# FFN stages that end on VectorE alone, and new engine costs in the planner that orders a Trainium2 kernel

## The chip, the cores and the metric

The kernel runs on one core of a Trainium2 chip. A core has five engines, each with an instruction queue of its own that it works off in order: TensorE (PE in the profile), VectorE (DVE), ScalarE (ACT), GpSimd (POOL) and SyncE (SP, which issues the transfers). The metric is the device time of one execution in microseconds, the median of several runs.

## The reference, cut to what matters

Four residual stages over a sequence of 1024 positions with 1024 features, all in float32: an FFN, a token mixer (two kinds of causal softmax attention), a second FFN, and then two layers on the sequence with 16 positions put ahead of it, an "even" layer (RG-LRU and SSD) and an "odd" one (stick-breaking attention).

```python
def swiglu(x, w_gate, w_up, w_down):
    return (jax.nn.silu(x @ w_gate) * (x @ w_up)) @ w_down      # 1024 -> 2816 -> 1024
...
f1 = swiglu(rms_norm(x, ffn1_pre_g[l]), ffn1_w_gate[l], ffn1_w_up[l], ffn1_w_down[l])
x = x + FFN_RESIDUAL_WEIGHT * rms_norm(f1, ffn1_post_g[l])
m = token_mixer(rms_norm(x, mix_pre_g[l]), w_in[l], ...)
x = x + rms_norm(m, mix_post_g[l])
f2 = swiglu(rms_norm(x, ffn2_pre_g[l]), ffn2_w_gate[l], ffn2_w_up[l], ffn2_w_down[l])
x = x + FFN_RESIDUAL_WEIGHT * rms_norm(f2, ffn2_post_g[l])
...
log_keep = jnp.where(before, jax.nn.log_sigmoid(-z), 0.0)       # odd layer, a block of 128 queries
csum = jnp.cumsum(log_keep, axis=-1)
weights = jnp.where(before, jnp.exp(jax.nn.log_sigmoid(z) + csum[..., -1:] - csum), 0.0)
```

## The kernel before, in words

Each float32 operand of a large product is split into a high and a low part (`wh` and `wl`, `Ah` and `Al`, `dh` and `dl`): ScalarE copies the high part, and another engine subtracts it for the low part. Three matmuls, lines 336 to 338 in `mm3`, then make one product.

The order of the instructions in every queue is decided while the program is built. Pieces of work are Python generators, called threads, which ask for an engine ("P", "A", "V", "G" for GpSimd, "D" for transfers) and give a cost in microseconds. `Sched.run` takes, again and again, the request with the smallest start time, then the smallest priority. The costs come from the functions `pe`, `act`, `dve` and `pool_tt`, and `HOP`, 0.45, is what it adds when work passes from one engine to another. So these numbers are no instructions; they decide which row stands ahead of which on each engine.

- **FFN stage** (`ffn_stage`, called twice). The products go by a seven-product scheme: `down` runs the products p of each chunk ci (0 to 2), with the result in `pdn` in PSUM. `evac_d` adds it into eight accumulators `acc` of 128x1024 (line 1104), some of the adds on GpSimd. `split_d` (line 1049) makes `dl`, the low parts of down's left operands. When an accumulator is complete, `post` takes its squares on ScalarE, gets `rs_y`, the inverse root, by small operations of 128x2 on VectorE (lines 306 to 310), multiplies by the gain `gp` (line 1220 in `scale`, on GpSimd for six of the eight, or line 1212) and adds the residual rows `xs` (line 1209, or 1215). `rows.put` stores the tile. The tiles are then normalized (line 603), transposed (`ptf`) and split into the next stage's `Ah` and `Al` (line 542).
- **`ahead`** is the stream that splits the next stage's first weights during an FFN's end; its subtraction (line 473 in `Stream.split`) is on GpSimd.
- **Mixer, even and odd stage.** Projections (`pe`, `pq`, `pk`, `pv`, `pg`) and attention or SSD chunks are emitted as threads beside each other, so that matmuls of the former stand between the waits of the latter. In the odd stage a block goes from scores `psc` (line 1500) over a scan of `kt` (line 2219), a product (line 2223), transposes `ptr` (line 1560) and their split `th`, `tl` (line 1511) to `po` (line 1543). In the even stage a chunk of the SSD goes from transposes `psx` to `xd` and `ab` on VectorE (lines 2703 and 2725), then to `psy`, `pso` and `pst` on TensorE; `sz` is a gate made from the projection `pe`. Outputs are projected by `pwo`.

Of the kernel before, what the change touches and what calls it, by code (L numbers as in the profile page):

```python
# [13 lines left out]
ALU = mybir.AluOpType  # L14
# [8 lines left out]
L = M + S  # L23
# [73 lines left out]
def act(n):  # L97
    return 0.07 + 0.92e-3 * n


def dve(n, speed=1):
    return 0.08 + 1.045e-3 * n / speed


def pool_tt(n):
    return 0.2 + 2.1e-3 * n

# [549 lines left out]
def ffn_stage(c, A, first, rows0, wg, wu, wd, gpost, res, rows, nxt, meta=None, cols=None):  # L657
# [6 lines left out]
    nc, tc, sch = c.nc, c.tc, c.sch  # L664
# [5 lines left out]
    with ExitStack() as ctx:  # L670
# [418 lines left out]
        def evac_d(ci, p, t, ps):  # L1089
# [22 lines left out]
            if p == 1:  # L1112
                if ci == 0:
                    yield from copy(c00, ps)
                    v = c01
                else:
                    yield from add(c00, c00)
                    v = yield from new_sg()
                vs[t] = v
                tt = yield from copy(v, ps)  # L1120
            elif p == 2:
                tt = yield from add(c00, c00)
            elif p == 6:
                v = vs[t]
                tt = yield from add(v, v)
            elif p == 7:
                v = vs[t]
                if ci == 0:
                    tt = yield from add(c10, v)
                else:  # L1130
                    yield from add(c01, c01, "G", v)
                    tt = yield from add(v, v)
            elif p == 4:
                tt = yield from add(c10, c10)
            elif p == 5:
                yield from add(c11, c11)
                tt = yield from add(c01, c01)
            else:
                tt = yield from add(c01, c01)
            r_mm.release(tt)  # L1140
            if p == 7:
                if ci == 0:
                    tt = yield from copy(c11, c10)
                else:
                    eng = "V" if ci == 2 else "G"
                    yield from add(c10, c10, eng, v)
                    tt = yield from add(c11, c11, "G", v)
                    r_sg.release(tt)
# [36 lines left out]
        def post(t, done):  # L1185
# [3 lines left out]
            nc.scalar.activation(junk(), acc[t], AF.Square, accum_out=ss[g][:, t - g:t - g + 1])  # L1189
            scaled = Ev()  # L1190
            on_pool = t not in (5, 7)
            if on_pool:
                sch.spawn(scale(t, scaled), 1, tt)
            left[g] = left.get(g, len(rows.members(t))) - 1
# [9 lines left out]
            r = rs[g][:, t - g:t - g + 1]  # L1204
            if on_pool:
                yield scaled
                yield ev_x[t]
                yield ("V", dve(1024))
                nc.vector.scalar_tensor_tensor(acc[t], acc[t], r, xs[t], op0=ALU.mult, op1=ALU.add)
            else:  # L1210
                yield ("V", dve(1024))
                nc.vector.scalar_tensor_tensor(acc[t], acc[t], r, gp[0], op0=ALU.mult, op1=ALU.mult)
                yield ev_x[t]
                yield ("V", dve(1024))
                nc.vector.tensor_add(acc[t], acc[t], xs[t])
            yield from rows.put(t, acc[t], junk)

        def scale(t, ev):
            t_ = yield ("G", pool_tt(1024))
            nc.gpsimd.tensor_mul(acc[t], acc[t], gp[0])  # L1220
            ev.set(t_)

# [74 lines left out]

        ahead = Stream(c, "G", shared=True)
        ahead.r_hl.free.clear()
# [417 lines left out]
def mixer_stage(c, A, rows0, prm, w_in, forget_b, lams, subln, rope, w_out, gpost, res, rows):  # L1717
# [3 lines left out]
    with ExitStack() as ctx:  # L1721
# [18 lines left out]
        def gate_evac(lf, tok, ps):  # L1740
# [17 lines left out]
            if tok is HALVES[1]:  # L1758
                cum = pm.tile([8, S], F32, tag="bc", name="cum", bufs=2)
                yield ("V", dve(1024))  # L1760
                nc.vector.tensor_tensor_scan(cum, c.one[:8].to_broadcast([8, S]), lf, 0.0, op0=ALU.mult, op1=ALU.add)
                t = yield ("D", 0.3)
                nc.sync.dma_start(cD, cum)
                r_bc.release(t + 1.0)
                r_bc.release(t + 1.0)
                T.event("cum").set(t + 2.0)
# [132 lines left out]
        def softmax(segs, m, pt, cb, ev, r):  # L1899
# [3 lines left out]
            for s, ps in enumerate(segs):  # L1903
                yield ("V", dve(m))
                if cb is not None:
# [7 lines left out]
            for s, ps in enumerate(segs):  # L1913
                t = yield ("A", act(m))
                nc.scalar.activation(pt[:, s * m:s * m + m], ps[:, :m], AF.Exp, bias=mx[:, 0:1], scale=-1.0,
                                     accum_out=sm[:, s:s + 1])
                T.r_ps["sc"].release(t)
            yield ("V", 0.2 * ns)
            if ns == 2:
# [214 lines left out]
def odd_stage(c, A, rows0, prm, w_in, w_out, res, final, out):  # L2134
# [3 lines left out]
    with ExitStack() as ctx:  # L2138
# [68 lines left out]
        def weights(ps, w, kt, k0, m, before, scanned, done):  # L2207
# [8 lines left out]

            t = yield ("V", dve(m))
            rev = kt[:, k0:k0 + m][:, ::-1]
# [224 lines left out]
def even_stage(c, A, rows0, prm, w_in, lru_wa, lru_wx, dt_bias, a_log, ssd_d, w_out, meta, res, rows):  # L2443
# [168 lines left out]
    def dt_rest():  # L2612
# [21 lines left out]
        nc.vector.tensor_scalar(l, dt, na, None, op0=ALU.mult)  # L2634
        yield ("V", dve(L))
        nc.vector.tensor_tensor_scan(ac, cut, l, 0.0, op0=ALU.mult, op1=ALU.add)
# [287 lines left out]
    def lru_rest(b, h, r, ig, t_, v):  # L2924
# [31 lines left out]
        for j in range(2):  # L2956
            u = 2 * b + j
            t = yield ("V", dve(LH, 0.5))
            nc.vector.tensor_tensor_scan(t_[:, j], r[:, j], v[:, j], 0.0 if h == 0 else carry[:, u:u + 1], op0=ALU.mult,
# [286 lines left out]
```

## Time and profile before

| | |
|---|---|
| median of 3 runs | 3675.97 us (3673.99 to 3686.52) |
| the profiled execution | 3678.58 us, span of its trace 3676.9 us |
| mean granted clock of TensorE | 0.978 of full speed |
| first FFN | 0 to about 705 us |
| mixer | to about 1350 us |
| second FFN | to about 2049 us |
| even stage | to about 2850 us |
| odd stage | to the end |

The span is the time from the first instruction to the last; 1.7 us of the run's time lie outside it. The stages follow one another, with the end of one over the start of the next. Since TensorE has most of the work, what matters of another engine is where TensorE stands still for it.

### The profile page before, as it was taken

The page shows a single profiled execution, that of the slowest core. Times are in us where ns is not written, and L with a number is a line of the kernel's source. Part 1 is how long each engine was busy: PE and PEld are TensorE (multiplying, and loading weights), DVE is VectorE, ACT ScalarE, POOL GpSimd, SP SyncE. Part 2 cuts the span into 40 slices and gives each one's busy share as a digit, 9 for nine tenths or more (in the row PEclk, how much of TensorE's full clock was granted, in tenths as well). Part 3 has the DMA queues.
Part 4 walks back from the last instruction along what each step waited for, and adds up shares of the span by engine and source line. Part 5 has one row for each costly group of instructions (what it writes and reads, how often), then busy time and mean ns, then how long its engine had stood idle before and what let it go on. Part 6 is the DMA issues. An engine that isn't in the chain of part 4 may idle for free. (4 is left out here: it accounts for less than half of the span.)

```text
span 3676.9 us, 51971 instructions
## 1 busy us (share of the span) xinstructions
PE 3469.4 (94%) x19675; PEld 2950.4 (80%) x19675; DVE 2756.6 (75%) x4900; ACT 1694.3 (46%) x3449; POOL 641.5 (17%) x577
## 2 busy tenths in 40 slices
PE   8899999799999899999999899998999999999989
PEld 7688888578878777888887899988878888888867
DVE  7876699977888769766799768568623788878784
ACT  4333244455656643333344437446412565656561
POOL 3211145411110114211354112113100000000000
PEclk9999999899999999999999999999999999999999
DMA  4232372311210342332561334234332111110123
GB/s 147 87 108 100 120 264 69 128 53 43 68 51 28 104 154 82 106 109 89 183 215 52 111 70 79 68 84 87 119 116 92 55 35 30 30 35 26 35 82 104
DMA packets 296627, 332.52 MB, mean 90 GB/s; under 512 B 17620, under 2 KB 220544, under 8 KB 296376
## 3 DMA queue, kind: packets, MB, share of 16 engines
q1 hardware_dynamic: 290584, 308.15, 27.6%
q10 hardware_dynamic: 5792, 21.04, 1.5%
q8 instruction: 155, 2.54, 0.3%
q14 instruction: 96, 0.79, 0.1%
HBM read 250.80 MB, written 78.35 MB: 90 GB/s over the span
## 5 line engine op out<-in xcount | busy, mean ns | idle before, releaser
L336 PE MATMUL pe<-Ah,wh 128*128 128x260 f32 (+1 forms) x1184 | 344.1, 291 | 21.6 <-ACT sz L224 7.5
L338 PE MATMUL pe<-Ah,wl 128*128 128x260 f32 (+1 forms) x1184 | 339.3, 287 | 0.0
L337 PE MATMUL pe<-Al,wh 128*128 128x260 f32 (+1 forms) x1184 | 339.0, 287 | 0.0
L224 ACT CAST wh<-w 128x512 fp32r<-128x512 f32 x280 | 162.5, 619 | 271.1 <-PE pst L337 193.0
L892 DVE TENSOR_TENSOR sg<-sg,pst 128x512 f32<-128x512 f32 x280 | 186.5, 682 | 114.6 <-PE pst L338 114.3
L337 PE MATMUL pst<-Al,wh 128*128 128x512 f32 x640 | 253.4, 396 | 2.2 <-DVE Al L815 2.2
L473 DVE TENSOR_TENSOR wl<-w,wh 128x512 fp32r<-128x512 f32 x280 | 209.9, 772 | 58.9 <-ACT wh L224 57.5
L336 PE MATMUL pst<-Ah,wh 128*128 128x512 f32 x640 | 251.8, 393 | 0.0
L338 PE MATMUL pst<-Ah,wl 128*128 128x512 f32 x640 | 251.6, 393 | 0.0
L337 PE MATMUL pdn<-dl,dh 128*128 128x512 f32 x592 | 233.4, 394 | 16.3 <-DVE dl L1049 16.3
L336 PEld LDWEIGHTS pe<-Ah,wh 128*128 128x128 f32 (+1 forms) x1184 | 225.8, 191 | 26.0 <-ACT sz L224 8.0
L1511 DVE TENSOR_TENSOR tl<-ptr,th 128x512 fp32r<-128x512 f32 (+2 forms) x344 | 198.0, 592 | 63.6 <-ACT th L224 61.2
L224 ACT CAST th<-ptr 128x512 fp32r<-128x512 f32 (+2 forms) x344 | 170.7, 515 | 133.4 <-PE ptr L1560 128.2
L338 PE MATMUL pdn<-dh,dl 128*128 128x512 f32 x592 | 231.7, 391 | 0.0
L336 PE MATMUL pdn<-dh 128*128 128x512 f32 x592 | 231.6, 391 | 0.0
L956 POOL TENSOR_TENSOR h<-h 128x512 f32<-128x512 f32 x88 | 134.5, 1529 | 535.6 <-DVE h L938 530.5
L337 PEld LDWEIGHTS pe<-Al,wh 128*128 128x128 f32 (+1 forms) x1184 | 225.7, 191 | 1.5 <-issue 0.5
L338 PEld LDWEIGHTS pe<-Ah,wl 128*128 128x128 f32 (+1 forms) x1184 | 225.5, 191 | 0.8
L2219 DVE TENSOR_TENSOR_SCAN kt<-kt,onec 128x392 f32<-128x392 f32 (+6 forms) x224 | 202.5, 914 | 26.1 <-ACT kt L224 25.0
L224 ACT CAST wh<-wr 128x1024 fp32r<-128x1024 f32 (+2 forms) x116 | 119.0, 1026 | 212.0 <-PE pwo L3045 121.7
L473 DVE TENSOR_TENSOR wl<-wr,wh 128x1024 fp32r<-128x1024 f32 (+1 forms) x110 | 138.8, 1263 | 86.0 <-ACT wh L224 85.7
L336 PE MATMUL pst<-T,wh 128*128 128x512 f32 x480 | 188.4, 395 | 10.9 <-ACT T L224 10.8
(555 smaller groups left out, 10496.0 us busy)
## 6 DMA issues: line engine op xcount, KB each, us to landing
hD<-h SPq DMA_DIRECT2D x22, 1792.0 KB
w<-in_ffn_w_gate_dram SPq DMA_DIRECT2D x20, 1024.0 KB
w<-in_ffn_w_up_dram SPq DMA_DIRECT2D x20, 1024.0 KB
d<-hD SPq DMA_DIRECT2D x18, 1024.0 KB
wr<-in_even_w_in_dram SPq DMA_DIRECT2D x36, 512.0 KB
wr<-in_odd_w_in_dram SPq DMA_DIRECT2D x32, 512.0 KB
wr<-in_w_in_dram SPq DMA_DIRECT2D x24, 512.0 KB
d<-in_ffn_w_down_dram SPq DMA_DIRECT2D x8, 1024.0 KB
```

What stands on the lines that cost most here:

```text
L224: self.last = _o(*a, **k)
L336: nc.tensor.matmul(ps, wh, xh, start=start, stop=False)
L337: nc.tensor.matmul(ps, wh, xl, start=False, stop=False)
L338: nc.tensor.matmul(ps, wl, xh, start=False, stop=stop)
L473: (nc.gpsimd if eng == "G" else nc.vector).tensor_sub(lo, raw, hi.bitcast(F32))
L892: nc.vector.tensor_add(dst, src, ps)
L956: nc.gpsimd.tensor_sub(q[:, o], q[:, a], q[:, b_])
L1511: nc.vector.tensor_sub(tl[:rows, :n], ptr[:rows, :n], th[:rows, :n].bitcast(F32))
L2219: nc.vector.tensor_tensor_scan(rev, rev, c.one.to_broadcast([P, m]), kt[:, k0 + m:k0 + m + 1], op0=ALU.mult, op1=ALU.mult)
```

## The change

The functions that give costs have new numbers, and the scans get a function of their own. At the end of both FFN stages no work is given to GpSimd: all eight tiles of `post` go the way that two went before, the adds of chunk 2 at p=7 go to VectorE, and so does the subtraction of `ahead`. The planner then runs with the new costs, so that the order of nearly all stages is another.

```diff
 def act(n):
-    return 0.07 + 0.92e-3 * n
+    return 0.16 + 0.87e-3 * n


 def dve(n, speed=1):
-    return 0.08 + 1.045e-3 * n / speed
+
+    return (0.15 if speed == 1 else 0.21) + 1.05e-3 * n / speed
+
+
+def scan(n):
+    return 0.22 + 2.08e-3 * n
+
+
+ACCUM = 0.19


 def pool_tt(n):
-    return 0.2 + 2.1e-3 * n
+    return 0.2 + 2.6e-3 * n
...
             elif p == 7:
                 v = vs[t]
+                eng = "V" if ci == 2 else "G"
                 if ci == 0:
                     tt = yield from add(c10, v)
                 else:
-                    yield from add(c01, c01, "G", v)
+                    yield from add(c01, c01, eng, v)
                     tt = yield from add(v, v)
...
                 else:
-                    eng = "V" if ci == 2 else "G"
                     yield from add(c10, c10, eng, v)
-                    tt = yield from add(c11, c11, "G", v)
+                    tt = yield from add(c11, c11, eng, v)
...
-            scaled = Ev()
-            on_pool = t not in (5, 7)
-            if on_pool:
-                sch.spawn(scale(t, scaled), 1, tt)
...
-            if on_pool:
-                yield scaled
-                yield ev_x[t]
-                yield ("V", dve(1024))
-                nc.vector.scalar_tensor_tensor(acc[t], acc[t], r, xs[t], op0=ALU.mult, op1=ALU.add)
-            else:
-                yield ("V", dve(1024))
-                nc.vector.scalar_tensor_tensor(acc[t], acc[t], r, gp[0], op0=ALU.mult, op1=ALU.mult)
-                yield ev_x[t]
-                yield ("V", dve(1024))
-                nc.vector.tensor_add(acc[t], acc[t], xs[t])
+            yield ("V", dve(1024))
+            nc.vector.scalar_tensor_tensor(acc[t], acc[t], r, gp[0], op0=ALU.mult, op1=ALU.mult)
+            yield ev_x[t]
+            yield ("V", dve(1024))
+            nc.vector.tensor_add(acc[t], acc[t], xs[t])
             yield from rows.put(t, acc[t], junk)
-
-        def scale(t, ev):
-            t_ = yield ("G", pool_tt(1024))
-            nc.gpsimd.tensor_mul(acc[t], acc[t], gp[0])
-            ev.set(t_)
...
-        ahead = Stream(c, "G", shared=True)
+        ahead = Stream(c, "V", shared=True)
...
-            t = yield ("V", dve(m))
+            t = yield ("V", scan(m))
             rev = kt[:, k0:k0 + m][:, ::-1]
             nc.vector.tensor_tensor_scan(rev, rev, c.one.to_broadcast([P, m]), kt[:, k0 + m:k0 + m + 1],
                                          op0=ALU.mult, op1=ALU.mult)
```

The other scans (`cum` of the mixer, `ac` and the LRU's `t_` of the even stage) get `scan` in the same way, and the softmax of the mixer has 0.14, `ACCUM` and 0.16 in its costs. By the order, GpSimd has 548 instructions instead of 582, VectorE 4920 instead of 4886, ScalarE three ACT table loads more (58), all in the even stage, and TensorE 19667 as before.

The first place is VectorE at the first FFN's end, where the last `dl` and the first tiles' `post` stand. Before:

```order
L308 SCALAR_TENSOR_TENSOR rs_a<-rs_y 128x2
L309 TENSOR_TENSOR rs_a<-rs_a,rs_v 128x2
L310 SCALAR_TENSOR_TENSOR rs_y<-rs_a,rs_y 128x2
L1209 SCALAR_TENSOR_TENSOR acc<-acc,rs_y,gp 128x1024
L1049 TENSOR_TENSOR dl<-d,dh 128x512
L308 SCALAR_TENSOR_TENSOR rs_a<-rs_y 128x2
L1209 SCALAR_TENSOR_TENSOR acc<-acc,rs_y,gp 128x1024
L1104 TENSOR_TENSOR acc<-acc,pdn 128x512
L309 TENSOR_TENSOR rs_a<-rs_a,rs_v 128x2
L1049 TENSOR_TENSOR dl<-d,dh 128x512
L310 SCALAR_TENSOR_TENSOR rs_y<-rs_a,rs_y 128x2
L1104 TENSOR_TENSOR acc<-acc,pdn 128x512
```

And of the change:

```order
L318 SCALAR_TENSOR_TENSOR rs_y<-rs_a,rs_y 128x2
L316 SCALAR_TENSOR_TENSOR rs_a<-rs_y 128x2
L1112 TENSOR_TENSOR acc<-acc,pdn 128x512
L317 TENSOR_TENSOR rs_a<-rs_a,rs_v 128x2
L1210 SCALAR_TENSOR_TENSOR acc<-acc,rs_y,gp 128x1024
L318 SCALAR_TENSOR_TENSOR rs_y<-rs_a,rs_y 128x2
L1210 SCALAR_TENSOR_TENSOR acc<-acc,rs_y,gp 128x1024
L1213 TENSOR_TENSOR acc<-acc,gp 128x1024 x2
L1210 SCALAR_TENSOR_TENSOR acc<-acc,rs_y,gp 128x1024 x2
L1213 TENSOR_TENSOR acc<-acc,d 128x1024 x2
L314 TENSOR_SCALAR rs_v<-ss 128x2
L1112 TENSOR_TENSOR acc<-acc,pdn 128x512 x4
```

The multiply by `gp` and the add of the residual are now two rows each on VectorE (L1210 and L1213) where GpSimd's product was ahead of one; the last `dl` (L1057) stands ahead of all of `post`. Behind these rows, up to the first `Al`, the order has two `wl` splits of 128x1024 and one of 128x64 that were GpSimd's, and one L1210 of a fifth tile.

The second place is TensorE in the even stage, at late chunks of the SSD (`psy`, `pso`, `pst` of one chunk, `psb` and `psx` of the next). Before:

```order
L2750 MATMUL psy<-ab,xd 64x128 x8
L2758 MATMUL pso<-xc_20290,S_21873 128x128 x4
L2763 MATMUL pst<-xe,bt 128x512
L2685 MATMUL psb<-xc_20290,xc_20113 128x128
L2686 MATMUL psb<-ident,xc_20113 128x128
L2691 MATMUL psx<-ident,xc_20748 128x128
L2691 MATMUL psx<-ident,xc_20749 128x128
L2691 MATMUL psx<-ident,xc_21656 128x128
L2691 MATMUL psx<-ident,xc_21657 128x128
L336 MATMUL pe<-Ah,wh 128x260
L337 MATMUL pe<-Al,wh 128x260
L338 MATMUL pe<-Ah,wl 128x260
```

And of the change:

```order
L2743 MATMUL psy<-ab,xd 64x128 x5
L2751 MATMUL pso<-xc_20276,S_21900 128x128 x4
L2756 MATMUL pst<-xe,bt 128x512
L2678 MATMUL psb<-xc_20276,xc_19962 128x128
L2679 MATMUL psb<-ident,xc_19962 128x128
L2684 MATMUL psx<-ident,xc_20824 128x128
L2684 MATMUL psx<-ident,xc_20825 128x128
L2684 MATMUL psx<-ident,xc_21652 128x128
L2684 MATMUL psx<-ident,xc_21653 128x128
L2743 MATMUL psy<-ab,xd 64x128 x8
L2751 MATMUL pso<-xc_20276,S_21900 128x128 x4
L2756 MATMUL pst<-xe,bt 128x512
```

Before, a chunk is followed by 48 rows of projections `pe` until the next `psy`; now the next chunk's `psy` stands right behind its `psx`, and so does the one after it.

The third place is TensorE in the odd stage, at the last projection `pg` of the kernel. Before:

```order
L338 MATMUL pg<-Ah,wl 128x512
L336 MATMUL pg<-Ah,wh 128x512
L337 MATMUL pg<-Al,wh 128x512
L338 MATMUL pg<-Ah,wl 128x512
L1543 MATMUL po<-th,v_31824 128x256
L1543 MATMUL po<-tl,v_31824 128x256
L1560 MATMUL ptr<-ident,pt 128x128 x3
L1543 MATMUL po<-th,v_31824 128x256
L1543 MATMUL po<-tl,v_31824 128x256
L1543 MATMUL po<-th,v_31824 128x256
L1543 MATMUL po<-tl,v_31824 128x256
L1500 MATMUL psc<-ks_32630,qs_25472 128x328
```

And of the change:

```order
L344 MATMUL pg<-Ah,wh 128x512
L345 MATMUL pg<-Al,wh 128x512
L346 MATMUL pg<-Ah,wl 128x512
L1536 MATMUL po<-th,v_31839 128x256
L1536 MATMUL po<-tl,v_31839 128x256
L1493 MATMUL psc<-ks_32632,qs_25475 128x328
L1494 MATMUL psc<-ks_32632,qs_25475 128x328
L1496 LDWEIGHTS identb
L1496 MATMUL psc<-mask_sb,identb 128x128
L1493 MATMUL psc<-ks_32632,qs_25475 128x328
L1494 MATMUL psc<-ks_32632,qs_25475 128x328
L1536 MATMUL po<-th,v_31839 128x256
```

The last `pg` has moved ahead: behind it stand 14 matmuls of `psc` by L1500 before, and 18 of the same line (L1493) now, 84 and 90 `po`, 72 and 78 `ptr`.

## Rows read from the trace of the kernel before

**Rows 1.** Page, section 1: busy time, share of the span, instructions.

```profile
PE 3469.4 (94%) x19675; PEld 2950.4 (80%) x19675; DVE 2756.6 (75%) x4900; ACT 1694.3 (46%) x3449; POOL 641.5 (17%) x577
```

**Rows 2.** Windows: length, busy us by engine (instructions), granted clock, DMA share, GB/s.

```profile
92.00:128.00 36.00, 23.91 (x87) 16.63 (x85) 35.19 (x50) 9.80 (x18) 10.71 (x7) 0.91 0.19 58
...
664.00:703.00 39.00, 27.26 (x108) 21.47 (x107) 38.71 (x51) 19.97 (x44) 20.98 (x9) 0.80 0.44 147
...
750.00:1345.00 595.00, 568.76 (x3367) 479.76 (x3367) 467.29 (x1187) 346.51 (x853) 82.55 (x50) 0.97 0.22 67
...
2049.00:2850.00 801.00, 763.96 (x5458) 694.34 (x5459) 497.24 (x855) 352.61 (x575) 103.75 (x138) 0.97 0.36 90
...
2850.00:3530.00 680.00, 636.69 (x4319) 561.19 (x4318) 535.93 (x946) 389.01 (x937) 17.61 (x137) 1.00 0.12 36
...
3534.00:3575.00 41.00, 28.06 (x145) 23.96 (x146) 39.47 (x61) 25.60 (x52) 0.40 (x4) 0.79 0.31 99
```

**Rows 3.** Timeline, TensorE, first FFN's end: start, us, name, [idle before <-releaser].

```profile
675.99 0.79 PE L337 MATMUL pdn<-dl,dh 128*128 128x512 f32 x1 [5.37 <-DVE dl L1049]
...
680.78 0.40 PE L336 MATMUL pdn<-op 128*128 128x512 f32 x1
...
720.75 0.40 PE L336 MATMUL pg<-Ah,wh 128*8 128x512 f32 x1 [4.28 <-ACT rx L224]
```

**Rows 4.** Timeline, GpSimd, the same place.

```profile
664.60 10.79 POOL L1220 TENSOR_TENSOR acc<-acc,gp 128x1024 f32<-128x1024 f32 x4 [5.42 <-ACT junk L224]
```

**Rows 5.** Groups by line and shape, VectorE, 664 to 703: busy, mean ns | idle.

```profile
L1049 DVE TENSOR_TENSOR dl<-d,dh 128x512 fp32r<-128x512 f32 x6 | 9.6, 1607 | 0.0
...
L308 DVE SCALAR_TENSOR_TENSOR rs_a<-rs_y 128x2 f32<-128x2 f32 x5 | 5.1, 1020 | 0.0
...
L306 DVE TENSOR_SCALAR rs_v<-ssp 128x2 f32<-128x2 f32 x3 | 4.8, 1600 | 0.0
...
L309 DVE TENSOR_TENSOR rs_a<-rs_a,rs_v 128x2 f32<-128x2 f32 x5 | 2.7, 548 | 0.1
...
L310 DVE SCALAR_TENSOR_TENSOR rs_y<-rs_a,rs_y 128x2 f32<-128x2 f32 x5 | 0.8, 154 | 0.1
```

**Rows 6.** Timeline, VectorE, the same place and just behind it.

```profile
665.66 4.70 DVE L1049 TENSOR_TENSOR dl<-d,dh 128x512 fp32r<-128x512 f32 x2
...
679.95 0.68 DVE L1049 TENSOR_TENSOR dl<-d,dh 128x512 fp32r<-128x512 f32 x1
...
702.30 1.40 DVE L542 SCALAR_TENSOR_TENSOR Al<-ptf,prm,Ah 128x512 fp32r<-128x512 f32 x2
...
710.03 1.22 DVE L1215 TENSOR_TENSOR acc<-acc,d 128x1024 f32<-128x1024 f32 x1
```

**Rows 7.** Timeline, GpSimd, second FFN's end.

```profile
2007.79 10.79 POOL L1220 TENSOR_TENSOR acc<-acc,gp 128x1024 f32<-128x1024 f32 x4 [5.42 <-ACT junk L224]
```

**Rows 8.** Timeline, VectorE, chunk adds of the first FFN.

```profile
654.45 1.78 DVE L1104 TENSOR_TENSOR acc<-acc,sg 128x512 f32<-128x512 f32 x1
```

**Rows 9.** Groups by line, odd stage 2850 to 3530, TensorE and VectorE.

```profile
L1543 PE MATMUL po<-tl,v 128*128 128x256 f32 x343 | 92.6, 299 | 30.2 <-DVE tl L1511 29.3
...
L2219 DVE TENSOR_TENSOR_SCAN kt<-kt,onec 128x392 f32<-128x392 f32 (+6 forms) x209 | 187.7, 907 | 26.1 <-ACT kt L224 25.0
...
L1511 DVE TENSOR_TENSOR tl<-ptr,th 128x512 fp32r<-128x512 f32 (+1 forms) x202 | 111.9, 569 | 40.0 <-ACT th L224 38.4
...
L2223 DVE TENSOR_TENSOR pt<-pt,kt 128x392 f32<-128x392 f32 (+5 forms) x209 | 102.9, 500 | 9.3
```

**Rows 10.** Timeline, even stage: TensorE's wait, then VectorE's part of one SSD chunk.

```profile
2572.86 0.58 PE L336 MATMUL pe<-Ah,wh 128*128 128x260 f32 x1 [4.56 <-ACT sz L224]
...
2585.82 0.68 DVE L2703 TENSOR_TENSOR xd<-psx,dT 128x512 f32<-128x512 f32 x1
...
2586.41 1.31 DVE L2725 TENSOR_TENSOR ab<-ab,cbm 128x1024 f32<-128x1024 f32 x1
```

**Rows 11.** Groups by line, ScalarE, whole run.

```profile
L243 ACT ACT_TABLE_LOAD x55 | 70.6, 1283 | 0.9
```

More of the change, by code (lines that the diff above doesn't have):

```diff
@@ L1759, in gate_evac @@
                 cum = pm.tile([8, S], F32, tag="bc", name="cum", bufs=2)
-                yield ("V", dve(1024))
+                yield ("V", scan(1024))
                 nc.vector.tensor_tensor_scan(cum, c.one[:8].to_broadcast([8, S]), lf, 0.0, op0=ALU.mult, op1=ALU.add)
@@ L1903, in softmax @@
             for s, ps in enumerate(segs):
-                yield ("V", dve(m))
+                yield ("V", dve(m) + (0.14 if cb is not None else 0))
                 if cb is not None:
@@ L1913, in softmax @@
             for s, ps in enumerate(segs):
-                t = yield ("A", act(m))
+                t = yield ("A", act(m) + ACCUM)
                 nc.scalar.activation(pt[:, s * m:s * m + m], ps[:, :m], AF.Exp, bias=mx[:, 0:1], scale=-1.0,
@@ L1917, in softmax @@
                 T.r_ps["sc"].release(t)
-            yield ("V", 0.2 * ns)
+            yield ("V", 0.16 * ns)
             if ns == 2:
@@ L2634, in dt_rest @@
         nc.vector.tensor_scalar(l, dt, na, None, op0=ALU.mult)
-        yield ("V", dve(L))
+        yield ("V", scan(L))
         nc.vector.tensor_tensor_scan(ac, cut, l, 0.0, op0=ALU.mult, op1=ALU.add)
@@ L2957, in lru_rest @@
             u = 2 * b + j
-            t = yield ("V", dve(LH, 0.5))
+            t = yield ("V", scan(LH))
             nc.vector.tensor_tensor_scan(t_[:, j], r[:, j], v[:, j], 0.0 if h == 0 else carry[:, u:u + 1], op0=ALU.mult,
```

## The prediction

> **What bounds the kernel now.** First the busy time of the engines over the whole run: TensorE works 3469.4 of 3676.9 us, VectorE 75%, ScalarE 46%, GpSimd 17% [rows 1]. Only some 200 us can be won by better order, and only where TensorE stands still. So next the table of stretches [rows 2]: in the first FFN's end (664 to 703) TensorE works 27.26 of 39 us while VectorE works 38.71; the start of the first FFN is the same picture (23.91 against 35.19 of 36). The mixer loses 26 us of 595 (568.76 busy), the even stage 37 of 801, the odd stage 43 of 680, and its tail 13 of 41, again with VectorE full (39.47). There the granted clock falls too: 0.80 at the FFN's end, 0.79 in the tail. VectorE is what TensorE waits for in all these places.
>
> Then the timeline of the FFN's end. TensorE waits 5.37 us for `dl` (L1049) up to 675.99, and 4.28 us at 720.75 for `rx` [rows 3]. In that wait GpSimd runs four multiplies of L1220 without a break, 10.79 us from 664.60 [rows 4]. VectorE's groups by shape say why it is late [rows 5]: six `dl` take 1607 ns each, where the same shape takes 0.68 us with GpSimd quiet [rows 6]; operations on 128x2, 0.15 us elsewhere (L310), average 1020 (L308), 1600 (L306) and 548 ns (L309). VectorE is held while GpSimd works on SBUF. The second FFN's end repeats it, with 10.79 us of L1220 [rows 7].
>
> [...]
>
> **The change, part by part.**
>
> *FFN ends, up to the next stage's first matmul.* VectorE works without a gap from 665.66 to the first `Al` (L542) at 702.30 [rows 6]: 36.6 us. Its excess over the unblocked price [rows 5, 6]: `dl` 9.6-6x0.68=5.5; L308 5.1-5x0.15=4.3; L306 4.8-3x0.15=4.3; L309 2.7-5x0.15=1.9; together 16.0. That goes with L1220 and GpSimd's lo splits. What is put before `Al` in VectorE's order: four adds L1213 at 1.22 us (L1215 is the same operation [rows 6]), 4.9; two `wl` splits of 128x1024, by the same row 2.4, and a small one of 0.15; one multiply L1210 more, by that row 1.2. Together 8.7. Net 7.3 us earlier, if VectorE stays busy throughout. Behind `Al` stand the rest: two more adds less the multiply that went ahead, 2.4-1.2=+1.2 before the wait of 4.28 us can end. So -6 per end, -12 for both. Bounds: the last `dl` also comes earlier, so VectorE may in turn wait for TensorE; if half the gain is lost so, -3. If the wait of 5.37 us and the slow clock behind it go in full and count in full (11 matmuls from 675.99 to 680.78 [rows 3], 4.8 us; if all that time ran at the lower of the two clocks, half of it, 2.4, is lost), -8 or -9. Range -6 to -18 for both.
>
> *Chunk adds of the FFN* (8 of 128x512 per stage). VectorE gets 8x0.6=4.8 us; its adds beside GpSimd's drop from 1.78 to 0.68 [rows 8]. TensorE has some 20 us of `pdn` matmuls of its own there: nothing on the path. If that cover went, 4.8 less some 3 of excess: +2.
>
> *The cost table.* It adds no instruction apart from three ACT table loads (58 against 55, 1283 ns [rows 11]) in the even stage; ScalarE is half idle there, and if uncovered they cost 3.8. What it does is to reorder, and I read that from the order, priced by the trace.
>
> - FFN starts: VectorE-bound [rows 2]. One difference of T goes from GpSimd to behind the stores of h, and `wl` splits go ahead of T's differences. Nothing tells a direction: 0, within 3 either way.
> - Mixer: the attention lies somewhat later behind the projections, and less `pwo` work is left for the last attention group. I counted 20 against 41 us of `pwo` matmuls behind it, still more than it can use. +1; -3 to +6.
> - Even stage: the second piece of the order shows two SSD chunks with no projection matmuls between them. A chunk's `psy` waits for `psx`, then `xd` 0.68 and `ab` 1.31 on VectorE [rows 10]: about 3 us from one to the next uncovered, so +6 for two, and a slow clock after it, 1 or 2. Before, those chunks had projections between, which waited 4.56 us for a `sz` [rows 10]; that wait may go, and others like it, since the projections now lie elsewhere. +2, the small remainder of +7 and -5; -8 to +10.
> - Odd stage: of the idle time, 30.2 us are at `po<-tl` [rows 9]: `tl` (L1511) stands behind scans of 907 ns. The new table knows that a scan costs twice as much as a product (0.22+2.08n), which should have the order leave room. But the third piece of the order shows the price: projections are emitted earlier, and behind the last `pg` there are 18 `psc` matmuls of L1500's kind left instead of 14, with 90 against 84 `po`. Nothing of another sort is left to fill with. One block's VectorE work is a scan 0.91, a product 0.50 and about one `tl` 0.57 [rows 9], 2 us; four more make 8 us, about half of it hidden since VectorE had been ahead of less: +4 in the tail. In the body I added up, stretch by stretch between projection groups, VectorE's work over TensorE's: such stretches become fewer but deeper (the largest 17 against 18 us as before, then 11 and 10 where there were 5). On the other hand, the mean distance from a `ptr` to its `po` grows from 2.3 to 2.5 us of matmul work. +1 for the body. Together +5; bounds -10 (a quarter of the 43 us goes) and +18 (the deeper stretches cost their whole depth, some 12 us more than before, and the tail 6).
>
> Sum: -12+0+1+2+5 = -4. The profiled execution took 3678.6 (span 3676.9 and 1.7 around it), so 3674.6; the median is 2.6 below that run, so **3672**.
>
> **Rivals.** A difference under 0.3%, 11 us, is about what a measurement of this kernel can't tell from none.
>
> 1. The forecast: the ends pay, the reordering eats a part: -11 to +4, 3665 to 3680. Chance 0.36.
> 2. The order pays too. A truer scan price empties the waits at `po<-tl` (a third of 30), and the waits for `sz` go: -12-10-8+2 (the mixer and the tail), -28, 3648. For it: the waits for `tl` are queueing behind scans that the old table priced at half. Against: VectorE is 79% busy in the odd stage [rows 2], and order cannot lessen its work. Chance 0.36 for anything faster than 11 us.
> 3. The other side: projections used up too early. Deep stretches and the tail cost +18, the bare SSD chunks +8, against -12: about +14, 3690. It decides from some +23 in the later stages. For it: the tail [rows 2], where TensorE already stands still for 13 of 41 us with nothing to fill. Chance 0.24.
> 4. VectorE isn't held by GpSimd at the ends: it then carries per stage six products' adds 7.3, eight chunk adds 4.8 and `wl` 2.6, and nothing goes: up to +15 per end uncovered, 3706. The rows of 128x2 operations of 2.3 us speak strongly against it. Chance 0.04.
>
> Faster by over 0.3%: 0.36 from rival 2. Slower: 0.28 from 3 and 4. Range 3647 to 3696, which leaves out the far parts of 2 and 3 and rival 4; the likeliest case's own is 3665 to 3683.
>
> **What would show it.** After the change, GpSimd should be empty at both FFN ends, no 128x2 operation on VectorE should take over 0.3 us there, the wait of 5.37 us before `pdn` should be under 2, and the first `pd` should start 5 to 9 us sooner, counted from the last FFN body. The pair of `psy` groups should show waits of 2 to 4 us each in the even stage; the last projection to first `pwo` of the odd stage should be about 4 us longer. The forecast is wrong if the even or the odd stage moves by over 10 us, or if the FFN's end shows VectorE waiting for ScalarE's squares or splits instead of running on.

## The result, and the profile after

The changed kernel takes 3715.45 us (median; 3711.62 to 3716.47), against 3676.26 for the kernel before in the same comparison: a ratio of 1.0099, 95% interval 1.0079 to 1.0119. The forecast was 3672 with a range to 3696. The profiled execution has a span of 3714.3 us, 37.4 more than before.

The busy times of the page, to be held against [rows 1]:

```profile
PE 3493.2 (94%) x19675; PEld 2967.0 (80%) x19675; DVE 2732.1 (74%) x4934; ACT 1701.0 (46%) x3452; POOL 583.0 (16%) x543
```

GpSimd has 58.5 us less to do, and VectorE is busy 24.5 us less although it has 34 instructions more: at the FFN's ends it is no longer held behind GpSimd (688 ns for a `dl` instead of 1607, fences below). TensorE has the same 19675 matmuls and is busy 23.8 us longer. Of the 37.4 us, then, only some 14 are waits; the larger part is the same work done more slowly, at a mean granted clock of 0.972 instead of 0.978.

Marks that both programs have tell where it happens (times in us from the start of the span, read from the first or last matmul of a name):

| mark | before | after | difference |
|---|---|---|---|
| last `pdn` of the first FFN ends | 692.1 | 684.1 | -8.1 |
| first `pd` (mixer) | 705.1 | 697.2 | -7.9 |
| last `pgu` (second FFN under way) | 1415.7 | 1408.6 | -7.2 |
| last `pdn` of the second FFN ends | 2035.3 | 2017.7 | -17.7 |
| first `pe` (even stage) | 2049.6 | 2033.6 | -16.0 |
| last `pe` | 2645.5 | 2658.6 | +13.1 |
| last `ptf` (odd stage) | 2876.7 | 2891.8 | +15.1 |
| last projection `pg` | 3529.2 | 3557.7 | +28.5 |
| last `po` | 3591.1 | 3618.8 | +27.7 |
| end | 3676.9 | 3714.3 | +37.4 |

Each FFN end gives some 8 us, the even stage takes 29 back and the odd one 22. The windows of these two stages (columns as in [rows 2]): first the kernel before, the even stage's projections, the odd stage whole, what lies behind its last `po`, and its body up to the last `pg`.

```profile
2049.60:2645.50 595.90, 563.37 (x4576) 541.43 (x4576) 425.70 (x731) 306.15 (x510) 98.95 (x136) 0.96 0.36 80
...
2876.70:3676.90 800.20, 734.52 (x4743) 640.83 (x4741) 612.91 (x1121) 427.63 (x1014) 13.95 (x131) 0.99 0.15 46
...
3591.10:3676.90 85.80, 76.58 (x330) 61.63 (x329) 41.02 (x130) 12.77 (x25) 0.00 (x0) 0.96 0.32 106
...
2876.70:3529.20 652.50, 610.47 (x4170) 539.66 (x4168) 519.56 (x913) 377.56 (x918) 13.45 (x126) 1.00 0.11 33
```

The same four of the changed kernel:

```profile
2033.60:2658.60 625.00, 572.55 (x4576) 549.35 (x4576) 415.82 (x728) 309.74 (x511) 112.23 (x136) 0.95 0.34 76
...
2891.80:3714.30 822.50, 754.70 (x4743) 655.47 (x4741) 612.13 (x1121) 428.81 (x1014) 14.02 (x131) 0.96 0.15 44
...
3618.80:3714.30 95.50, 86.31 (x372) 69.47 (x371) 44.37 (x134) 15.07 (x28) 0.00 (x0) 0.96 0.32 106
...
2891.80:3557.70 665.90, 622.62 (x4149) 548.36 (x4147) 513.46 (x905) 374.42 (x906) 13.43 (x125) 0.98 0.11 31
```

In the even stage both columns move for one count of matmuls (4576): TensorE is busy 572.55 instead of 563.37, and stands still 52.5 instead of 32.5. In the odd stage (4743 matmuls in both) TensorE stands still 67.8 instead of 65.7, hardly more, and is busy 20.2 us longer; the granted clock is 0.96 instead of 0.99. Behind the last `po` 372 matmuls are left instead of 330, 9.7 us more.

**The FFN's end.** VectorE's groups from 656 to 695, to be read beside [rows 5], then the first `Al` in its timeline beside [rows 6], then TensorE's waits there beside [rows 3]:

```profile
L1057 DVE TENSOR_TENSOR dl<-d,dh 128x512 fp32r<-128x512 f32 x11 | 7.1, 688 | 0.2 <-ACT dh L232 0.2
...
L317 DVE TENSOR_TENSOR rs_a<-rs_a,rs_v 128x2 f32<-128x2 f32 x5 | 0.8, 154 | 0.0
```

```profile
694.45 5.35 DVE L550 SCALAR_TENSOR_TENSOR Al<-ptf,prm,Ah 128x512 fp32r<-128x512 f32 x8
```

```profile
687.28 2.85 PE L562 MATMUL ptf<-ident,gp 128*128 128x128 f32 x12 [3.20 <-DVE gp L611]
...
697.22 0.79 PE L344 MATMUL pd<-Ah,wh 128*128 128x512 f32 x1 [3.21 <-DVE Al L550]
...
712.42 0.39 PE L344 MATMUL pg<-Ah,wh 128*8 128x512 f32 x1 [2.35 <-ACT rx L232]
```

A `dl` takes 688 ns instead of 1607 and an operation of 128x2 0.15 us. `Al` begins at 694.45, 7.85 us earlier. The wait of 5.37 us before `pdn` is gone; what is left are 3.20 and 3.21 us where TensorE has no matmuls of the FFN any more and VectorE's last adds and norms lie ahead, and 2.35 us before `pg` instead of 4.28.

**The even stage.** TensorE at the SSD chunks that the order had left without projections (the second place of the change's section):

```profile
2571.56 0.60 PE L2684 MATMUL psx<-ident,xc 128*128 128x128 f32 x4
...
2581.39 1.97 PE L2743 MATMUL psy<-ab,xd 128*64 128x128 f32 x16 [9.23 <-DVE ab L2718]
...
2586.05 0.60 PE L2684 MATMUL psx<-ident,xc 128*128 128x128 f32 x4
...
2590.64 1.34 PE L2743 MATMUL psy<-ab,xd 128*64 128x128 f32 x16 [3.99 <-DVE ab L2718]
...
2601.04 0.58 PE L344 MATMUL pe<-Ah,wh 128*128 128x260 f32 x1 [4.98 <-ACT sz L232]
```

From `psx` to the next `psy` TensorE waits 9.23 us, and 3.99 us a chunk later; then `pe` waits 4.98 us for a `sz`. VectorE in the first of these waits:

```profile
2573.61 1.51 DVE L2947 TENSOR_TENSOR v<-v,ig 128x1040 f32<-128x1040 f32 x1
...
2575.04 0.68 DVE L2696 TENSOR_TENSOR xd<-psx,dT 128x512 f32<-128x512 f32 x1
...
2575.64 2.64 DVE L2952 TENSOR_TENSOR_SCAN t<-r,carry,v 128x520 f32<-128x520 f32 x2
...
2578.21 1.99 DVE L481 TENSOR_TENSOR wl<-wor,wh 128x1024 fp32r<-128x1024 f32 x1
...
2580.12 1.21 DVE L2718 TENSOR_TENSOR ab<-ab,cbm 128x1024 f32<-128x1024 f32 x1
```

The chunk's `xd` stands behind a multiply of the LRU (1.51 us), and `ab`, which `psy` needs, behind two scans of the LRU and a weight split: 2.64 and 1.99 us. So the chain from `psx` to `psy` isn't `xd` and `ab` but all that stands between them in VectorE's queue. ScalarE at the same time, from which the next projections wait for `sz`:

```profile
2573.89 1.06 ACT L232 ACTIVATE ab<-ab 128x1024 f32<-128x1024 f32 x1
...
2583.30 0.63 ACT L232 ACTIVATE ea<-ea 128x512 f32<-128x512 f32 x1 [8.35 <-DMA ea<-aD]
...
2598.67 0.63 ACT L232 ACTIVATE ea<-ea 128x512 f32<-128x512 f32 x1 [7.11 <-DMA ea<-aD]
...
2600.60 0.94 ACT L232 ACTIVATE sz<-pe 128x260 f32<-128x260 f32 x3
```

It waits 8.35 and then 7.11 us for `ea`, a transfer, and the `sz` that frees the PSUM buffer of the next `pe` stands behind the second of these and a table load of 1.28 us. So the projections that come after the bare chunks can't start at once either.

**The odd stage.** TensorE's group with the largest wait, to be read beside [rows 9]:

```profile
L1536 PE MATMUL po<-tl,v 128*128 128x256 f32 x339 | 95.0, 307 | 22.6 <-DVE tl L1504 21.9
```

It waits less there than before (22.6 against 30.2). But look at one of these waits and what follows it (`pv` matmuls ahead of it, `po` behind, all of 256 columns):

```profile
2956.46 0.28 PE L1478 MATMUL pv<-wh,Ah 128*128 128x256 f32 x1
...
2956.58 0.28 PE L1479 MATMUL pv<-wl,Ah 128*128 128x256 f32 x1
...
2959.63 0.39 PE L1536 MATMUL po<-tl,v 128*128 128x256 f32 x1 [2.52 <-DVE tl L1504]
...
2962.77 0.41 PE L1536 MATMUL po<-th,v 128*128 128x256 f32 x1
...
2962.99 0.41 PE L1536 MATMUL po<-tl,v 128*128 128x256 f32 x1
```

```profile
2960.00:2963.40 3.40, 3.40 (x15) 2.87 (x13) 3.06 (x6) 1.69 (x3) 0.00 (x0) 0.50 0.31 80
...
2964.20:2968.00 3.80, 3.30 (x23) 2.70 (x22) 3.66 (x6) 3.75 (x11) 0.00 (x0) 1.00 0.02 6
```

Ahead of the wait such matmuls start 0.12 us apart, behind it 0.22 us. The windows say why: the granted clock is 0.50 from 2960.0 to 2963.4, the lower of the two levels that this trace's record of the clock holds (0.50 and 1.00), and 1.00 again behind that. In the kernel before, a wait of 1.66 us in the same stage has no such trail:

```profile
3037.53 0.39 PE L1543 MATMUL po<-tl,v 128*128 128x256 f32 x1 [1.66 <-DVE tl L1511]
...
3037.76 0.28 PE L336 MATMUL pk<-Ah,wh 128*128 128x256 f32 x1
...
3037.88 0.28 PE L337 MATMUL pk<-Al,wh 128*128 128x256 f32 x1
```

Behind the idle 1.66 us of the last fence the clock did not fall: that trace has no time at 0.50 in the whole body of the stage. Over the stage's body the changed kernel has a granted clock of 0.98 and the one before 1.00, with 43.3 and 42.0 us of idle time.

One trace tells the size of this only roughly. Runs 1, 4 and 11 below have the odd stage's order of before, runs 2, 3, 5 and 6 that of the change, and the body (from the last `ptf` to the last `pg`) came out like this (each trace records when the clock changed):

| order | traces | body, us | idle, us | waits of 2 us or more | at the lower clock, us |
|---|---|---|---|---|---|
| of before | before, runs 1, 4, 11 | 652.2 to 653.3 | 42.0 to 42.4 | none | 0, 0, 3.4, 0 |
| of the change | change, runs 2, 3, 5, 6 | 662.4 to 665.9 | 43.3 to 46.3 | 6 in each | 27.3, 20.5, 23.9, 10.2, 17.1 |

So the new order makes the body 9 to 14 us longer. Against the trace of before 1 to 4 of them are idle, and 6 to 12 are longer busy time, in each of the five traces about half of its time at the lower clock (12.2 of 27.3, 9.1 of 20.5, 10.9 of 23.9, 5.7 of 10.2, 8.5 of 17.1). How much that is differs between executions of one order.

### The profile page after: what moved, and what is told of

Read it like the earlier page. It is cut to its first block, busy times and chain, and to the rows that moved or that the text cites. A ratio compares the mean times of both kernels' runs of the same rounds, so it can differ in the third digit from the quotient of the medians.

```text
span 3714.3 us, 51935 instructions
## 1 busy us (share of the span) xinstructions
PE 3493.2 (94%) x19675; PEld 2967.0 (80%) x19675; DVE 2732.1 (74%) x4934; ACT 1701.0 (46%) x3452; POOL 583.0 (16%) x543
## 5 line engine op out<-in xcount | busy, mean ns | idle before, releaser
L481 DVE TENSOR_TENSOR wl<-wr,wh 128x1024 fp32r<-128x1024 f32 (+2 forms) x116 | 143.7, 1239 | 118.7 <-ACT wh L232 118.5
L2212 DVE TENSOR_TENSOR_SCAN kt<-kt,onec 128x392 f32<-128x392 f32 (+5 forms) x224 | 202.2, 913 | 14.3 <-ACT kt L232 13.2
```

The lines of the kernel that those rows point to most:

```text
L481: (nc.gpsimd if eng == "G" else nc.vector).tensor_sub(lo, raw, hi.bitcast(F32))
L2212: nc.vector.tensor_tensor_scan(rev, rev, c.one.to_broadcast([P, m]), kt[:, k0 + m:k0 + m + 1], op0=ALU.mult, op1=ALU.mult)
```

## The experiments

All times are medians; each ratio is to the kernel before on the same chip, with its 95% interval.

**1. The FFN ends alone.** The change's code, with the old table in every stage (a global, set ahead of each stage, chooses between the two):

```diff
+OLD = False
...
 def act(n):
-    return 0.16 + 0.87e-3 * n
+    return 0.07 + 0.92e-3 * n if OLD else 0.16 + 0.87e-3 * n
...
+    globals()["OLD"] = True
     A1 = ffn_stage(...)
```

From run 5 on the global is `NEW`, a list of the functions that have their new costs.

> The FFN ends of the change (all eight tiles, the chunk adds and the next weights' low parts on VectorE) with the old cost table in every stage, so that the order of the even and the odd stage is that of before. Theory A (the ends pay, the new order of the even and the odd stage loses it): the first pd and the first pe come 8 us sooner each, the rest keeps its length: 3656 to 3661, ratio to before about 0.9955. Rival B (the ends pay only with the new table's order around them, or move a cost into the stages behind): 3668 or more.

3664.38 us, ratio 0.9965 (0.9952 to 0.9978). Between what A and B had said by its median, but the marks decide: first `pd` 8.0 us earlier, first `pe` 18.2 earlier, and the even and odd stages as long as before:

```profile
2031.40:2625.60 594.20, 562.15 (x4576) 540.12 (x4576) 424.62 (x725) 305.95 (x508) 105.35 (x136) 0.97 0.35 80
...
2859.30:3511.60 652.30, 609.90 (x4169) 539.37 (x4168) 519.37 (x913) 377.36 (x917) 13.39 (x126) 1.00 0.11 33
```

**2. The table alone** (the kernel before, with the new cost functions).

> The new cost table alone, with the FFN ends of before (GpSimd multiplies six tiles). Theory A: the loss of the even and the odd stage stays whole and the gain at the ends is gone: 3715 plus 16 to 18, so 3728 to 3735. Rival B (GpSimd's absence is what hurts later stages): close to before, 3676 to 3690.

3735.80, ratio 1.0160 (1.0145 to 1.0175). Just above the upper edge of theory A's 3728 to 3735; rival B is out. The two edits are worth -12 and +59 alone, and +39 together, so they nearly add up (+47), with some 8 us left: without the new ends the table also costs at the FFN's ends (first `pd` 4.9 us later than before, first `pe` 9.9).

**3. The change with the old table in the even stage.**

> The change, with the old cost table in the even stage alone; its order is then that of before, all other stages have the order of the change. Theory A: the 29 us between the first pe and the last go, 3684 to 3688. Rival C (it is the three added loads of the activation table, 1.28 us each): only 4 us go with them, 3710 or so. Rival D (the even stage loses because of the state in which the FFN leaves it): no change, 3715.

3680.10, ratio 1.0010 (1.0000 to 1.0019): 35 us off by the medians and 33 by the ratios, some 4 to 6 more than theory A's 29, with the even stage's part in the trace at 31.5. The even stage is back, the odd one stays long:

```profile
2033.80:2627.30 593.50, 560.56 (x4576) 538.68 (x4576) 426.60 (x728) 306.01 (x508) 99.84 (x136) 0.97 0.36 80
...
2858.60:3524.20 665.60, 621.30 (x4149) 547.34 (x4147) 513.68 (x905) 374.05 (x906) 13.43 (x125) 0.98 0.11 31
```

C is out: the loads could not give back more than 4 us. D is out too.

**4. The change with the old table in the odd stage.**

> The change, with the old cost table in the odd stage alone; its order is then that of before. Theory A: the 22 us from the odd stage's start to the end go, 3692 to 3695, and the time at the lower clock in that stage falls from some 63 us to some 25. Rival (the odd stage is longer since the even stage hands it its tiles in another order): no change, 3715.

3691.64, ratio 1.0038 (1.0024 to 1.0052): 24 us off, or 22 by the ratios. The time at the lower clock in the whole odd stage fell from 61 us to 31.

```profile
2033.60:2655.30 621.70, 569.13 (x4576) 546.14 (x4576) 415.67 (x728) 309.67 (x512) 111.94 (x136) 0.95 0.34 76
...
2886.60:3539.90 653.30, 611.24 (x4170) 540.66 (x4168) 519.57 (x913) 377.41 (x917) 13.43 (x126) 1.00 0.11 33
```

The even stage is as long as in the change and the odd body as before (653.3 us, 42.1 idle, clock 1.00). Each stage's loss thus comes from its own order.

**5 and 6. Which costs strip the SSD's chunks bare.** In the even stage only `dve` is new, or `act` and `dve`.

> The change, where in the even stage only dve has its new cost (act, scan and pool_tt the old ones). The order of the even stage is new nearly everywhere, but no SSD chunk stands bare: at least 24 projection matmuls lie between psx and the next psy. Theory A (the bare chunks late in the stage make its loss): the even stage is as long as before's, 3680 to 3690. Rival E (any new order of this stage loses, being tuned to the old one): 3700 or more.

> The change, where in the even stage act and dve have new costs and scan and pool_tt the old ones. Only with both new do two chunks stand bare, as in the change. Theory A: as slow as the change, 3710 to 3718, with the loss between the last 100 us of psy. Rival E': it is the price of scan or pool_tt that does it: 3690 or less.

3684.33, ratio 1.0013 (1.0004 to 1.0023), and 3715.06, ratio 1.0093 (1.0078 to 1.0108). The stage's projections, with `dve` new and then with both:

```profile
2033.20:2628.60 595.40, 560.95 (x4576) 538.85 (x4576) 422.28 (x728) 315.05 (x515) 101.15 (x136) 0.97 0.35 80
```

```profile
2032.50:2657.20 624.70, 572.06 (x4576) 548.83 (x4576) 415.18 (x728) 307.23 (x509) 111.25 (x136) 0.95 0.34 76
```

And TensorE's waits in the second:

```profile
2580.03 1.98 PE L2749 MATMUL psy<-ab,xd 128*64 128x128 f32 x16 [9.23 <-DVE ab L2724]
...
2589.30 1.30 PE L2749 MATMUL psy<-ab,xd 128*64 128x128 f32 x16 [3.98 <-DVE ab L2724]
```

The times are theory A's: a new order with projections between the chunks costs nothing (595.4 against 595.9), one with two bare chunks costs 29 us, and the waits of 9.23 and 3.98 are those of the change. The new price of scans and of GpSimd isn't needed for it. But the waits at `psy` can't be the whole cause. Summed over the stage (us, times, longest), first in the change, then in run 5:

```profile
PE psy L2743 <- DVE ab L2718: 15.7, 4, 9.2
```

```profile
PE psy L2749 <- DVE ab L2724: 15.0, 6, 5.8
```

Run 5 waits nearly as long there, in shorter pieces, and loses nothing. What the change has beyond it are above all waits for `sz`, at `pe` and at `pga` (the LRU's gate projections): 18.2 us, against 4.2 in run 5 and 15.1 in the kernel before. Most of the loss does lie where the bare chunks stand: in the stage's last 125 us TensorE stands still for 24.5 at a clock of 0.89, in the last 96 us of the kernel before for 8.2 at 0.95. But the orders differ elsewhere too, and no run put projections back between those two chunks alone, so their own price is not shown.

**7 and 8. The odd stage with new prices for some functions.** Old table elsewhere, new ends.

> The FFN ends of the change with the old table everywhere (3664 in a run before), but for the odd stage, where act and scan have new costs. In its order the longest stretches of attention matmuls with no projection between are 5.9 us (before 6.1, the change 8.8), and behind the last pg stand 29 psc matmuls instead of 34 (44 in the change). Theory F (the length of the stretches without projections decides, through the waits and the clock after them): as fast as with the old table or a little faster, 3656 to 3664, with 25 us or less at the lower clock in the odd stage. Rival G (the truer price of a scan costs time here whatever the stretches are): 3672 or more.

> As the run with act and scan, but in the odd stage only scan has its new cost. The order then has five stretches of 8.2 to 8.8 us without projections, as the change has, and 29 psc matmuls behind the last pg, fewer than before. Theory F: the body of the odd stage is 6 to 12 us longer through waits of 2 us and the clock after them, the tail some 3 shorter: 3667 to 3674. Rival H (the odd stage's loss is the tail behind the last pg): 3658 to 3664.

3666.12, ratio 0.9961 (0.9947 to 0.9975), and 3667.88, ratio 0.9966 (0.9953 to 0.9979): within the intervals no different from run 1. In the traces the bodies of the stage differ, the first at 662.4 us and a clock of 0.98, the second at 655.4 and 1.00:

```profile
2853.70:3516.10 662.40, 619.76 (x4185) 550.25 (x4183) 522.75 (x919) 379.40 (x922) 13.50 (x127) 0.98 0.11 32
```

```profile
2862.40:3517.80 655.40, 617.03 (x4188) 544.67 (x4188) 521.75 (x922) 380.74 (x923) 13.55 (x127) 1.00 0.11 33
```

Theory F fails: the order with the shortest stretches (7) has the longer body and loses to the clock (47 us at the lower clock in the odd stage, where theory F had 25 or less), the one with the long stretches (8) hardly does. Counting matmuls between projections does not tell the waits. Nor does the tail give back what the body loses: from the last `pg` to the end these two take 146.3 and 148.8 us, run 1 148.3, and the whole odd stage is 808.8 and 804.3 us against run 1's 800.6. The timed medians don't show these 4 to 8 us; the stages ahead of it, with one order, differ by up to 9 us between these three traces.

**9 and 10. More work for VectorE, in lumps or spread.** In run 1's kernel, repeats of `tl`'s subtraction, here those of run 9:

```diff
         nc.vector.tensor_sub(tl[:rows, :n], ptr[:rows, :n], th[:rows, :n].bitcast(F32))
+        if self.nt == 9 and n == 512:
+            self.count = getattr(self, "count", 0) + 1
+            for _ in range(3 if self.count in (20, 40, 60, 80, 100, 120, 140, 160) else 0):
+                nc.vector.tensor_sub(tl[:rows, :n], ptr[:rows, :n], th[:rows, :n].bitcast(F32))
```

> The FFN ends of the change with the old table everywhere (3664), plus 24 idle repeats of the subtraction that makes tl in the odd stage (0.57 us each, 13.7 us of VectorE), in eight lumps of three, so that eight waits before po<-tl grow by up to 1.7 us. The result stays the same. Theory K (what costs in the odd stage of the change is not more idle time but that it comes in longer pieces, each followed by a spell at the lower clock): besides 8 to 13 us more idle time some 20 to 27 us more at the lower clock, which cost half of that: 3682 to 3690. Rival L (the clock doesn't depend on how the idle time is cut): as the run with the same repeats spread, 3670 to 3678.

> The same 24 repeats, one each at 24 places of the odd stage. Theory K: waits grow by up to 0.57 us each; at most 10 us more at the lower clock; 5 to 13 us longer than without: 3669 to 3677. Rival L: the same time as the run in lumps, within 3 us.

3664.68, ratio 0.9960 (0.9946 to 0.9973), and 3664.40, 0.9959 (0.9944 to 0.9974): no loss that the intervals could show, so nothing was told apart. Nor were these the edits that had been meant: the counter doesn't get to 100 in this stage, so that only 12 of the 24 repeats are in either program (4946 instructions on VectorE instead of 4934), in four lumps or at twelve places. The longest waits of the body were those of run 1 (1.9 us and less); the repeats stood where TensorE had other work. Yet in both traces the clock fell, for 13.7 and 10.2 us of a body that takes 658.0 and 656.7 us, against none of 652.3 in run 1's. Run 9:

```profile
2857.10:3515.10 658.00, 615.83 (x4170) 544.85 (x4168) 527.25 (x925) 377.88 (x917) 13.31 (x126) 0.99 0.11 32
```

**11. Only `post` on VectorE**, with the chunk adds and the next weights' low parts on GpSimd.

> Old table everywhere; of the FFN ends only the multiply and the add of post are all on VectorE, and the adds of chunk 2 and the low parts of the next weights are as before (one of the adds was on VectorE before too). If the multiplies of L1220 hold up most: 3665 to 3669, a gain of 4 us or so at each end against 8 with all three moved; if the three low-part subtractions on GpSimd (2.8 us each) matter as much, 3669 or more.

3673.47, ratio 0.9988 (0.9979 to 0.9997): a third of the gain by the ratios. The marks give more, 5.6 us at the first end and 4.9 at the second, and the stretch between them took 4.9 us longer than before, which stays open. TensorE, GpSimd and VectorE at the first FFN's end:

```profile
680.78 0.80 PE L351 MATMUL pdn<-dl,dh 128*128 128x512 f32 x1 [6.54 <-DVE dl L1063]
```

```profile
670.10 4.75 POOL L487 TENSOR_TENSOR wl<-wr,wh 128x1024 fp32r<-128x1024 f32 x2 [10.86 <-ACT wh L238]
```

```profile
670.16 2.37 DVE L322 SCALAR_TENSOR_TENSOR rs_a<-rs_y 128x2 f32<-128x2 f32 x1 [1.06 <-ACT rs_y L238]
```

GpSimd's two splits, 4.75 us together, now hold VectorE: an operation of 128x2 beside them takes 2.37 us, and TensorE waits 6.54 us for a `dl` behind it. The last `pdn` ends at 692.2, as in the kernel before. So the multiplies are only a part of the gain; what the chunk adds and the splits are worth each was not told apart.

**12. A planner that believes in shorter chains.**

> The FFN ends of the change, the old table, and HOP 0.3 instead of 0.45 in every stage: a planner that believes in shorter chains where the change believes in longer ones. In its order the stretches of attention without projections are shorter (4.5 against 6.1 us), 24 psc are left behind the last pg instead of 34, and no SSD chunk stands bare (48 projection matmuls at the least before the last). If longer believed chains are what pushes the fillers ahead: 3655 to 3663; if the old value of 0.45 is at its best: 3668 or more.

3677.68, ratio 1.0000 (0.9991 to 1.0009): some 13 us worse than run 1, in spite of an order with shorter stretches. The odd stage's body takes 672.8 us in its trace (run 1: 652.3) and stands still for 50.2. By this sign too, the count of stretches is no guide. The new `HOP` changes the other stages as well, so the 13 us aren't the odd stage's alone.

**13 and 14. The same test as 9 and 10, on the waits themselves.**

> The FFN ends of the change with the old table everywhere (3664), plus 32 idle repeats of tl's subtraction in the odd stage (128x256, some 0.28 us each, 9 us of VectorE), four behind each of the eight tl for which TensorE waited longest there (1.3 to 1.9 us). The result stays the same. Theory K (idle time in longer pieces is followed by spells at the lower clock, and these cost in the odd stage of the change): eight waits of 2.3 to 3 us, 9 us more idle time, and six to eight more spells of 3.4 us at the lower clock, 10 to 14 us: 3680 to 3688. Rival L (the clock has another cause): 9 us more at the most, 3668 to 3674.

> The same, but the 32 repeats stand in pairs behind the sixteen tl for which TensorE waited next longest (0.4 to 1.24 us), 11 us of VectorE as some are wider. Theory K: sixteen waits of 1 to 1.8 us, 11 us more idle time and few spells at the lower clock: 3672 to 3678, shorter than with the lumps although the added work is more. Rival L: as with the lumps or longer.

3673.43, ratio 0.9986 (0.9977 to 0.9995), and 3671.25, ratio 0.9982 (0.9973 to 0.9990). The body of the odd stage, first with lumps, then spread:

```profile
2855.90:3523.20 667.30, 621.26 (x4170) 548.00 (x4168) 530.07 (x945) 378.15 (x917) 13.29 (x126) 0.98 0.11 32
```

```profile
2855.10:3523.00 667.90, 622.77 (x4170) 549.10 (x4170) 532.63 (x947) 379.46 (x917) 13.32 (x126) 0.98 0.11 32
```

Against run 1's body (652.3 us, 609.90 busy, clock 1.00) both are 15 us longer, and idle 46.0 and 45.1 us against 42.4: of the 10.7 and 13.3 us that VectorE works longer only 3 or 4 show as waits, and 11 to 13 as longer busy time at a clock of 0.98. By the ratios the step is 8 and 6 us (run 1's profiled execution was the shortest of its runs), and by the medians both times lie in rival L's band. But the two runs don't tell K from L, since their waits hardly differ: the lumps made three of over 2 us (2.63, 2.38 and 2.37) instead of eight, and the spread repeats made three as well (2.12, 2.11 and 2.11). And L's account of 9 us of added work doesn't fit either: what grew in the traces is not so much the waits as the time at the lower clock, 27.3 us in each.

All sixteen traces together say more, since they record every fall of the clock. In the odd stage's body there are 60 falls, and 59 of them began during a wait of 1 us or more or within 4 us behind it, stretches that make 11% of the time. A fall came during the wait or within 2 us of its end for 27 of the 43 waits of 2 us or more, for 22 of the 121 from 1.2 to 2 us, and for 16 of the 337 from 0.5 to 1.2. That is the core of theory K: the longer wait is more often followed by a fall. It is no certainty, since the same wait of the same order is followed by one in one execution and not in another.

## Why the prediction was wrong

**FFN ends, -12 (range -6 to -18): right.** The marks give -16 at the first `pe` in the change and -18 in run 1, the timed runs of run 1 a median of -12. `Al` came 7.85 us earlier where the sum said 7.3, for the reason given: GpSimd's hold on VectorE went with its work. Rival 4 is out: `dl` fell from 1607 to 688 ns. Why GpSimd's work holds VectorE is shown by no run here. The small term of +1.2 behind `Al` did not show.

**FFN starts 0, mixer +1: right.** From the first `pd` to the last `pgu` +0.7. The traces can't tell this from nothing: with one order this stretch differs by some 5 us between them (707.4 to 712.8 in the runs with the new ends and the old table, without 11 and 12).

**Even stage +2: the failing step.** The place was named and the mechanism too, the size was not: two chunks at "about 3 us from one to the next", +6 and 1 or 2 for the clock, less 5 for waits that might go. It cost 29, 20 of them idle. Three parts of the sum were wrong. The chain from `psx` to `psy` was priced by its own two operations, `xd` 0.68 and `ab` 1.31, but in VectorE's queue the LRU's scans and a weight split stand between them, and the wait was 9.23. The slow clock was 9 us, the growth of busy time, not 1 or 2. And the credit for `sz` did not come: the waits for it grew from 15.1 to 18.2 us over the stage, among them 4.98 at `pe`, behind ScalarE's waits for transfers of `ea`. Run 3 shows that the 29 us belong to this stage's order; how they divide among the bare chunks and the rest is only argued from the traces. The order of VectorE could have been read for this very chunk as it was for the FFN's end.

**Odd stage +5 (bound +18): the second failing step.** The body was given +1 from two counts that pulled in different ways; it lost 13.4 us (652.5 to 665.9), with only 1.3 more of idle time, and 9 to 14 us over five traces of its order. The sum knew TensorE's idle time as the one way to lose, and gave the clock no term here because it stood at 1.00 [rows 2]. It had no look at how long single waits become: the new order has six of 2 us or more and the old none, with 10 to 27 us at the lower clock instead of 0 to 3.4. The tail's +4 was the right sign at the wrong place: from the last `pg` to the last `po` nothing is lost (61.9 and 61.1 us), but 42 matmuls of `pwo` that had filled it before are left for the end, 9.7 us.

**The rivals.** The third came true in its direction ("projections used up too early", +14), but with +39: its point of decision, +23 in the later stages, was passed by far with 51. The second failed: the waits at `po<-tl` did fall, from 30.2 to 22.6, as it said, and brought nothing. The range was made of bounds that both late stages passed, 29 against 10 and 22 against 18. By the prediction's own sign, a late stage that moves by over 10 us, the forecast was wrong in both.

What stays open: what decides whether a given wait is followed by a fall of the clock in the odd stage, and how much of the loss the six long waits make. The sum of the waits doesn't settle it (nearly the same before and after), their length does in part, and no run here took the waits of the change away one by one.

The best version measured is run 1, the FFN ends with the old table, 0.35% faster than before (0.22 to 0.48); runs 7 to 10 can't be told from it.

## What to carry to other kernels

A planner's table made truer is not a better order: it orders by where it believes that chains end, and what counts is which work is left to fill the waits; read the new order on every engine at the places where one engine feeds another, and price a chain by all that stands in those queues. Where TensorE is as busy as here (94% of the span), ask of each stage how long its single waits are, and not only how much they add up to: with 1 to 4 us more of idle time, but six waits of 2 us or more where there had been none, one stage here became 9 to 14 us longer. An elementwise operation that looks cheap on GpSimd must be charged with what VectorE loses beside it (here a `dl` took 1607 ns instead of 688), and taking only some of them away left TensorE's wait for `dl` in place (run 11).

## What was not expected of the hardware

Operations of two elements on 128 partitions, which read next to nothing, were held beside GpSimd's work nearly as long as large ones: 1600 and 1020 ns on average, where a `dl` of 128x512 took 1607 [rows 5], 2.37 us for one in run 11, and 0.15 us without it. And in the odd stage the clock fell when VectorE got some 11 to 13 us of work more in 650, though the idle time hardly rose: a clock of 1.00 and 609.90 us busy without, 0.98 and 621.26 us with the lumps. One order of instructions spent between 10 and 27 us at the lower clock there, from one execution to the next.
